# Convolution layer: the 31 taps shared out differently among TensorE, VectorE, ScalarE and GpSimd

## The chip, the core and the metric

The kernel runs on one core of a Trainium2 chip. The metric is the device time of one launch in microseconds; the median of the timed runs counts. Engines are named as in the profile: PE (TensorE, with PEld for its weight loads), DVE (VectorE), ACT (ScalarE), POOL (GpSimd) and SP (which issues the weight DMAs).

## The reference, cut to what matters

The model is six layers over 512 tokens of width 1024: attention, convolution, latent attention, attention, a three-branch mixer and a feed-forward layer. The change lies in the convolution layer alone:

```python
def _conformer_conv(h, w_in, b_in, conv_w, conv_b, ln_g, ln_b, w_out):
    proj = h @ w_in + b_in
    a, b, gate = jnp.split(proj, 3, axis=-1)
    u = a * jax.nn.sigmoid(b)
    u = lax.conv_general_dilated(          # B_CONV = 31 taps, causal, one filter per channel
        u, conv_w[:, None, :].astype(u.dtype), window_strides=(1,),
        padding=[(B_CONV - 1, 0)], dimension_numbers=('NWC', 'WIO', 'NWC'),
        feature_group_count=B_WIDTH) + conv_b
    u = jax.nn.silu(_layer_norm(u, ln_g, ln_b))
    return (u * jax.nn.silu(gate)) @ w_out
```

Each of the 1024 channels is convolved with its own 31 weights, then a layer norm runs over all channels of a token. So nothing of the norm can start before every channel's convolution is done.

## The kernel before

**Arithmetic.** Every large matmul is done in three passes on pairs of rounded halves (`mm3`, high*high, high*low, low*high), all recorded at L195. A weight unit comes by DMA as `wr`; ACT rounds it to `wh` (L53) and, in this layer, POOL subtracts to get the low half `wl` (L60, because `k.share(B_SPLIT)` is 1.0 from the second pair of channels on).

**The convolution layer.** Channels lie on partitions in eight chunks of 128, tokens along the free dimension. `pair(p)` makes `u` for chunks 2p and 2p+1: first the `b` half (sigmoid, L1088), then the `a` half times it (L1093).

- Seven chunks (all but 3) are convolved by `conv(c)`. DVE multiplies and adds tap by tap into a PSUM bank (`tp`, two banks): one L1034 and then n-1 times L1036. The remaining taps are made by ACT as scaled copies (`tmp`, and the first one directly in `acc`, L1040) and added up by POOL (L1042). At the end DVE adds both sums into `y[:, c]` (L1043). n is `B_VECTOR` = 23 for chunks 0 to 6 and `B_LAST` = 20 for chunk 7. The pool has three `acc` and five `tmp` buffers.
- Chunk 3 goes through PE. ACT makes two 128x128 diagonal matrices for each tap (`dh`, `dl`, L1057 and L1058), and PE accumulates 31 taps x 3 matmuls in one bank (`conv_on_tensor`), which ACT copies to `y` with the bias (L1079).

**What sets the order.** A scheduler orders the instructions of each engine ahead of time with a simulated clock: of those ready, the one with the smallest priority number goes first, and each engine then runs its list in that order. Numbers grow along the program. `k.low()` adds a million to them, and `conv(c)` is issued inside it, so a weight split of POOL goes ahead of a tap of the seven chunks. `conv_on_tensor` and the weight stream are outside it.

**After the convolution.** The gate projection (`gates`, 192 matmuls) fills PE while the norm's chain runs. Its order on PE is written out (`manual_schedule`): the channel mean of chunks 0 to 5 (`mean(0, 6)`) comes 22 us of matmul time into the gates, that of chunks 6 and 7 (`mean(6, 8)`) 10 us later, with 24 gate matmuls between the two. After it come `centre` (ACT copies the mean, L1132; DVE and POOL subtract it, L1138 and L1136; ACT squares, L1141; DVE and POOL add, L1150 and L1145), `square` (L1159) and `scale`, each at its place among the gate matmuls.

```python
        flow.later(B_CONV - 10.0, lambda: mean(0, 6))
        flow.later(B_CONV, lambda: mean(6, 8))
        with tc.manual_schedule(engines={mybir.EngineType.PE}):
            for p in range(4):
                k.lin_fm(gates(p))
            flow.need(lambda: "pr" in st)
```

Of the kernel before, what the change touches and what calls it, by code (L numbers as in the profile page):

```python
# [12 lines left out]
AF = mybir.ActivationFunctionType  # L13
ALU = mybir.AluOpType
# [956 lines left out]


B_TAPS = 31
B_VECTOR = 23
B_LAST = 20
B_TENSOR = (3,)
B_CONV = 32.0
B_SQUARE = 7.0
B_POOL = (2, 5)
# [16 lines left out]

def layer_b(k, j, gnext, out=None, on_vector=B_VECTOR, on_tensor=B_TENSOR):
    nc, tc, ins, flow = k.nc, k.tc, k.ins, k.flow
    with ExitStack() as ctx:
# [4 lines left out]
        def wt(n, bufs, nmn, dt=F32):  # L1004
            return work.tile([P, n], dt, tag=nmn, name=k.nm(nmn), bufs=bufs)

        cols, turn1 = k.columns(one, work, [(ins["b_b_in"][j], 24), (ins["b_conv_b"][j], 8), (ins["b_ln_g"][j], 8), (ins["b_ln_b"][j], 8)])
        taps, turn2 = k.tap_columns(one, work, ins["b_conv_w"][j], B_TAPS)
        cb, lg, lb = cols[:, 24:32], cols[:, 32:40], cols[:, 40:48]
# [9 lines left out]
        PAD = 32  # L1019
        u = one.tile([P, 8, PAD + S], F32, tag="u", name=k.nm("u"))  # L1020
        y = one.tile([P, 8, S], F32, tag="y", name=k.nm("y"))
# [5 lines left out]
        tap = lambda a, i: a[:, PAD - B_TAPS + 1 + i : PAD - B_TAPS + 1 + i + S]  # L1027

        def conv(c):

            n = on_vector if c < 7 else B_LAST
            wc = lambda i: taps[:, c, i : i + 1]
            ps = k.bank("tp")
            nc.vector.tensor_scalar(out=ps, in0=tap(u[:, c], 0), scalar1=wc(0), scalar2=cb[:, c : c + 1], op0=ALU.mult, op1=ALU.add)  # L1034
            for i in range(1, n):
                nc.vector.scalar_tensor_tensor(out=ps, in0=tap(u[:, c], i), scalar=wc(i), in1=ps, op0=ALU.mult, op1=ALU.add)  # L1036
            acc = wt(512, 3, "acc")
            for i in range(n, B_TAPS):
                tmp = acc if i == n else wt(512, 5, "tmp")
                nc.scalar.activation(out=tmp, in_=tap(u[:, c], i), func=AF.Copy, scale=wc(i))  # L1040
                if i > n:
                    nc.gpsimd.tensor_tensor(out=acc, in0=acc, in1=tmp, op=ALU.add)  # L1042
            nc.vector.tensor_tensor(out=y[:, c], in0=ps, in1=acc, op=ALU.add)  # L1043

        diag, halves = {}, {}

        def diagonal(c, i):

            if "w" not in halves:
                w = halves["w"] = wt(2 * B_TAPS, 1, "wc").rearrange("p (i n) -> p i n", i=2)  # L1050
                wr = wt(B_TAPS, 1, "wr", F32R)
                nc.scalar.activation(out=wr, in_=taps[:, c], func=AF.Copy)
                nc.vector.tensor_scalar(out=w[:, 0], in0=wr.bitcast(F32), scalar1=1.0, scalar2=None, op0=ALU.mult)
                nc.vector.tensor_tensor(out=w[:, 1], in0=taps[:, c], in1=w[:, 0], op=ALU.subtract)
            w = halves["w"]
            dh, dl = diag[i] = wt(P, 8, "dh", F32R), wt(P, 8, "dl", F32R)
            nc.scalar.activation(out=dh, in_=k.ident, func=AF.Copy, scale=w[:, 0, i : i + 1])  # L1057
            nc.scalar.activation(out=dl, in_=k.ident, func=AF.Copy, scale=w[:, 1, i : i + 1])  # L1058

        def begin_on_tensor(c, ps):  # L1060

            halves["u"] = uh, ul = wt(PAD + S, 1, "uh", F32R), wt(PAD + S, 1, "ul", F32R)
            for a in (uh, ul):
                nc.scalar.activation(out=a[:, 0:PAD], in_=u[:, c, 0:PAD], func=AF.Copy)
            k.split(ps, uh[:, PAD:], ul[:, PAD:])
            with k.low():
                for i in range(8):
                    diagonal(c, i)

        def conv_on_tensor(c):  # L1070

            uh, ul = halves["u"]
            ps = k.bank("lin")
            for i in range(B_TAPS):
                if i not in diag:
                    diagonal(c, i)
                k.mm3(ps, *diag[i], tap(uh, i), tap(ul, i), i == 0, i == B_TAPS - 1)
                flow.pump()
            nc.scalar.activation(out=y[:, c], in_=ps, func=AF.Identity, bias=cb[:, c : c + 1])  # L1079

        def pair(p):
            sig = {}

            def on_b(c, ps):
                flow.need(lambda: ready)
                sig[c] = wt(512, 3, "sig")
                i = 8 + 2 * p + c
                k.table("sig", nc.scalar.activation(out=sig[c], in_=ps, func=AF.Sigmoid, bias=cols[:, i : i + 1]))  # L1088

            def on_a(c, ps):  # L1090
                i = 2 * p + c
                dst = ps if i in on_tensor else u[:, i, PAD:]
                nc.vector.scalar_tensor_tensor(out=dst, in0=ps, scalar=cols[:, i : i + 1], in1=sig[c], op0=ALU.add, op1=ALU.mult)  # L1093
                if i in on_tensor:
                    begin_on_tensor(i, ps)
                else:
                    with k.low():
                        conv(i)

            return [(k.h_opnd, 8, on_b), (k.h_opnd, 8, on_a)]  # L1100
# [15 lines left out]
        for c in on_tensor:  # L1116
            conv_on_tensor(c)
# [4 lines left out]
        def mean(a, b):  # L1122
            if a == 0:
                st["pm"] = k.bank("sc")
            for c in range(a, b):
                k.mm(st["pm"], ones, y[:, c], c == 0, c == 7)
            if b == 8:
                centre()
# [38 lines left out]
# [4 lines that stand above are left out]
# [514 lines left out]
```

## Time and profile before

| | us |
|---|---|
| median of 3 runs | 2039.26 (2038.92 to 2047.69) |
| the profiled execution: its time | 2043.2 |
| its span, first to last instruction | 2041.4 |
| the convolution's taps in it, first to last POOL add | 345.3 to 459.8 |
| layer norm and the rest of the gates | up to about 492 |

The profile is of one execution, so its stretches are compared with its own span. Times in the rows are us from the start of the span, and ns where a mean is given. A busy PE is not a PE at its peak, since matmuls overlap: what counts is how far apart they start.

### The profile page before, as it was taken

Reading aid. Unit: us, or ns where it says so; the run is one execution under the profiler, and the core shown is the slowest. Engines: PE = TensorE matmul, PEld = TensorE weight load, DVE = VectorE, ACT = ScalarE, POOL = GpSimd, SP = SyncE. Lnnn points to the kernel's source line nnn. Section 1 sums busy time; section 2 is a strip of 40 time slices with the busy share of each in tenths; the row PEclk is TensorE's granted clock in tenths of the full one; section 3 lists DMA queues with packets and bytes.
Section 4 is the critical chain, followed back from the end, with each engine's and each line's share of the span. In section 5 each row is a group of like instructions: output and inputs, shape, how many; then the busy total and the mean of one; then the engine's idle time right before and its main releaser. Section 6 shows DMA issues by size and latency. Waiting matters only on the chain.

```text
span 2041.4 us, 27224 instructions
## 1 busy us (share of the span) xinstructions
PE 1988.7 (97%) x9875; PEld 1663.7 (81%) x9875; DVE 1172.4 (57%) x2185; ACT 996.7 (49%) x2107; POOL 915.0 (45%) x812
## 2 busy tenths in 40 slices
PE   8999999999999999999999999999999999999999
PEld 6787888887898887877778888888888888888887
DVE  6677766995456656786665678747624433221321
ACT  5555646574465645555554776546423333222220
POOL 6666624993455417775535444102511223333331
PEclk9899999999999999999999999999999999999999
DMA  6122142323331323221423122322334244333331
GB/s 199 45 83 83 42 145 89 122 62 116 106 100 43 104 74 107 65 83 42 140 88 100 59 82 73 93 83 69 118 102 136 93 125 144 93 100 97 100 96 52
DMA packets 161095, 191.54 MB, mean 94 GB/s; under 512 B 15917, under 2 KB 131997, under 8 KB 160960
## 3 DMA queue, kind: packets, MB, share of 16 engines
q1 hardware_dynamic: 160960, 189.80, 29.6%
q8 instruction: 78, 1.28, 0.3%
q14 instruction: 57, 0.47, 0.1%
HBM read 177.18 MB, written 12.58 MB: 93 GB/s over the span
## 4 chain that ended last, share of the span: by engine, by line
PE 81%; DVE 6%; POOL 5%; ACT 3%; issue 2%; DMA 2%; SPq 0%; DVEq 0%; ACTq 0%; POOLq 0%
PE lin L195 71%; PE sc L195 4%; PE tp L195 3%; PE tp L303 2%; DVE wl L60 1%; POOL st L217 1%; PE lin L303 1%; POOL wl L60 1%; DMA wr<-in_a_w_in_dram 1%; POOL m L461 1%; ACT wh L53 1%; POOL m L460 1%; DVE m L580 1%; DVE st L644 0%; ACT w L638 0%
## 5 line engine op out<-in xcount | busy, mean ns | idle before, releaser
L60 POOL TENSOR_TENSOR wl<-wr,wh 128x1024 fp32r<-128x1024 f32 (+2 forms) x151 | 364.8, 2420 | 506.4 <-ACT wh L53 490.9
L53 ACT ACTIVATE wh<-wr 128x1024 fp32r<-128x1024 f32 (+2 forms) x306 | 318.6, 1044 | 376.1 <-PE lin L195 230.7
L195 PE MATMUL lin<-hh,wh 128*128 128x512 f32 (+1 forms) x928 | 350.1, 379 | 3.3 <-ACT hh L353 3.3
L195 PE MATMUL lin<-hl,wh 128*128 128x512 f32 (+1 forms) x928 | 350.1, 378 | 0.0
L195 PE MATMUL lin<-hh,wl 128*128 128x512 f32 (+1 forms) x928 | 349.2, 377 | 0.0
L195 PE MATMUL lin<-wh,hh 128*128 128x512 f32 (+2 forms) x864 | 332.9, 387 | 1.9 <-DVE sg L602 0.7
L195 PE MATMUL lin<-wl,hh 128*128 128x512 f32 (+2 forms) x864 | 329.2, 382 | 1.1 <-DVE wl L60 1.1
L195 PE MATMUL lin<-wh,hl 128*128 128x512 f32 (+2 forms) x864 | 330.1, 382 | 0.1
L60 DVE TENSOR_TENSOR wl<-wr,wh 128x1024 fp32r<-128x1024 f32 (+3 forms) x155 | 211.4, 1367 | 188.9 <-ACT wh L53 188.1
L195 PEld LDWEIGHTS lin<-hh,wh 128*128 128x128 f32 x928 | 175.7, 190 | 35.3 <-ACT hh L353 3.6
L195 PEld LDWEIGHTS lin<-hl,wh 128*128 128x128 f32 x928 | 175.9, 190 | 31.6 <-issue 0.5
L195 PEld LDWEIGHTS lin<-hh,wl 128*128 128x128 f32 x928 | 175.9, 190 | 31.2
L195 PEld LDWEIGHTS lin<-wh,hh 128*128 128x128 f32 x864 | 165.0, 191 | 29.0 <-PE tp L303 0.9
L195 PEld LDWEIGHTS lin<-wl,hh 128*128 128x128 f32 x864 | 165.2, 191 | 27.8 <-DVE wl L60 2.2
L195 PEld LDWEIGHTS lin<-wh,hl 128*128 128x128 f32 x864 | 164.8, 191 | 27.2 <-DVE hl L354 0.4
L195 PE MATMUL lin<-wh,ot 128*128 128x512 f32 x384 | 129.9, 404 | 1.2 <-ACT ot L680 1.0
L217 POOL TENSOR_TENSOR st<-st,minus_half 128x8 f32<-128x8 f32 (+4 forms) x109 | 115.5, 1061 | 7.6 <-DVE st L1159 2.3
L468 DVE TENSOR_TENSOR x<-lin,x 128x512 f32<-128x512 f32 x80 | 54.3, 687 | 102.3 <-PE lin L195 101.9
L1036 DVE SCALAR_TENSOR_TENSOR tp<-u,taps,tp 128x512 f32<-128x512 f32 x151 | 104.0, 754 | 1.1
L638 ACT ACTIVATE w<-sc,st 128x128 f32<-128x128 f32 (+3 forms) x128 | 67.0, 524 | 71.8 <-DVE st L637 71.0
L195 PEld LDWEIGHTS lin<-wh,ot 128*128 128x128 f32 x384 | 71.3, 188 | 16.1 <-ACT ot L680 2.1
L1042 POOL TENSOR_TENSOR acc<-acc,tmp 128x512 f32<-128x512 f32 x52 | 66.7, 1301 | 22.4 <-ACT tmp L1040 21.4
(321 smaller groups left out, 3814.8 us busy)
## 6 DMA issues: line engine op xcount, KB each, us to landing
wr<-in_a_w_in_dram SPq DMA_DIRECT2D x128, 256.0 KB
wr<-in_w_in_dram SPq DMA_DIRECT2D x48, 512.0 KB
wr<-in_b_w_in_dram SPq DMA_DIRECT2D x24, 512.0 KB
wr<-in_w_branch_dram SPq DMA_DIRECT2D x24, 512.0 KB
wr<-in_w_ffn_gate_dram SPq DMA_DIRECT2D x22, 512.0 KB
wr<-in_w_ffn_up_dram SPq DMA_DIRECT2D x22, 512.0 KB
wr<-in_w_ffn_down_dram SPq DMA_DIRECT2D x22, 512.0 KB
xs<-x SPq DMA_DIRECT2D x40, 256.0 KB
```

What stands on the lines that cost most here:

```text
L53: nc.scalar.activation(out=hi, in_=raw, func=AF.Copy)
L60: eng.tensor_tensor(out=lo, in0=raw, in1=hi.bitcast(F32), op=ALU.subtract)
L195: self.nc.tensor.matmul(out=out, lhsT=lhsT, rhs=rhs, start=start, stop=stop)
L217: self.nc.gpsimd.tensor_tensor(out=y, in0=ms, in1=self.minus_half.to_broadcast(list(ms.shape)), op=ALU.pow)
L303: self.nc.tensor.transpose(tp[:, c], a, self.ident)
L460: nc.gpsimd.tensor_tensor(out=mv, in0=rv, in1=bc(cs), op=ALU.mult)
L461: nc.gpsimd.tensor_tensor(out=m, in0=m, in1=tmp, op=ALU.add)
L468: self.nc.vector.tensor_tensor(out=xs, in0=ps, in1=xs, op=ALU.add)
L580: nc.vector.tensor_tensor(out=mv, in0=mv, in1=r.unsqueeze(2).to_broadcast([P, 8, 64]), op=ALU.mult)
L638: nc.scalar.activation(out=e[:, m, :n], in_=sc[:, :n], func=AF.Exp, bias=mx[:, m : m + 1], accum_out=sums[:, 2 * m + h : 2 * m + h + 1],)
L1036: nc.vector.scalar_tensor_tensor(out=ps, in0=tap(u[:, c], i), scalar=wc(i), in1=ps, op0=ALU.mult, op1=ALU.add)
L1042: nc.gpsimd.tensor_tensor(out=acc, in0=acc, in1=tmp, op=ALU.add)
```

## The change

TensorE's chunk gets 24 taps as diagonals instead of 31. The other seven are made as for the other chunks, by ACT and POOL: `rest(c, n)` is the old ACT and POOL loop of `conv` as a function, called for chunk 3 outside `k.low()`. For that the chunk's `u` is needed in SBUF too, so ACT copies it from the bank. The last step of chunk 3 is now one DVE instruction that adds bank, bias and `acc`. The seven other chunks lose a tap on DVE each (23 to 22, and 20 to 19 for chunk 7), which goes to ACT and POOL.

```diff
-B_VECTOR = 23
-B_LAST = 20
+B_VECTOR = 22
+B_LAST = 19
 B_TENSOR = (3,)
+B_DIAGONAL = 24
...
             for i in range(1, n):
                 nc.vector.scalar_tensor_tensor(out=ps, in0=tap(u[:, c], i), scalar=wc(i), in1=ps, op0=ALU.mult, op1=ALU.add)
+            nc.vector.tensor_tensor(out=y[:, c], in0=ps, in1=rest(c, n), op=ALU.add)
+
+        def rest(c, n):
+
             acc = wt(512, 3, "acc")
             for i in range(n, B_TAPS):
                 tmp = acc if i == n else wt(512, 5, "tmp")
-                nc.scalar.activation(out=tmp, in_=tap(u[:, c], i), func=AF.Copy, scale=wc(i))
+                nc.scalar.activation(out=tmp, in_=tap(u[:, c], i), func=AF.Copy, scale=taps[:, c, i : i + 1])
                 if i > n:
                     nc.gpsimd.tensor_tensor(out=acc, in0=acc, in1=tmp, op=ALU.add)
-            nc.vector.tensor_tensor(out=y[:, c], in0=ps, in1=acc, op=ALU.add)
+            return acc
...
             k.split(ps, uh[:, PAD:], ul[:, PAD:])
+            nc.scalar.activation(out=u[:, c, PAD:], in_=ps, func=AF.Copy)
...
-            for i in range(B_TAPS):
+            acc = rest(c, B_DIAGONAL)
+            for i in range(B_DIAGONAL):
                 if i not in diag:
                     diagonal(c, i)
-                k.mm3(ps, *diag[i], tap(uh, i), tap(ul, i), i == 0, i == B_TAPS - 1)
+                k.mm3(ps, *diag[i], tap(uh, i), tap(ul, i), i == 0, i == B_DIAGONAL - 1)
                 flow.pump()
-            nc.scalar.activation(out=y[:, c], in_=ps, func=AF.Identity, bias=cb[:, c : c + 1])
+            nc.vector.scalar_tensor_tensor(out=y[:, c], in0=ps, scalar=cb[:, c : c + 1], in1=acc, op0=ALU.add, op1=ALU.add)
```

## Rows read from the trace of the kernel before

**Rows 1.** The page's busy times by engine: us, share of the span, instructions.

```profile
PE 1988.7 (97%) x9875; PEld 1663.7 (81%) x9875; DVE 1172.4 (57%) x2185; ACT 996.7 (49%) x2107; POOL 915.0 (45%) x812
```

**Rows 2.** Chain that ended last, convolution to norm: start, length, what.

```profile
459.93 5.15 PE sc L195 x12
465.07 5.50 PE lin L195 x24
470.57 1.72 PE sc L195 x4
...
479.43 1.24 POOL acc L1145
```

**Rows 3.** Windows over the taps: length, busy time of each engine, clock.

```profile
345.33:459.78 114.45, 114.45 (x518) 94.83 (x517) 110.95 (x165) 79.50 (x137) 110.73 (x72) 1.00 0.28 88
```

**Rows 4.** Groups on POOL, DVE and ACT in that stretch: count, busy, mean.

```profile
L1042 POOL TENSOR_TENSOR acc<-acc,tmp 128x512 f32<-128x512 f32 x52 | 66.7, 1301 | 22.4 <-ACT tmp L1040 21.4
L60 POOL TENSOR_TENSOR wl<-wr,wh 128x1024 fp32r<-128x1024 f32 x20 | 48.2, 2415 | 1.6 <-ACT wh L53 1.6
L1043 DVE TENSOR_TENSOR y<-tp,acc 128x512 f32<-128x512 f32 x7 | 4.8, 687 | 0.1
L1040 ACT ACTIVATE tmp<-u,taps 128x512 f32<-128x512 f32 x52 | 35.7, 713 | 4.5 <-POOL acc L1042 4.3
```

**Rows 5.** Timeline of PE: first taps of chunk 3, the two means, the square.

```profile
414.16 0.39 PE L195 MATMUL lin<-uh,dh 128*128 128x512 f32 x1
414.39 0.39 PE L195 MATMUL lin<-ul,dh 128*128 128x512 f32 x1
...
480.71 1.95 PE L195 MATMUL sc<-ones,acc 128*128 128x1 f32 x16 [0.90 <-POOL acc L1145]
```

**Rows 6.** Timeline of POOL: one double split, then the end of the taps.

```profile
352.95 4.79 POOL L60 TENSOR_TENSOR wl<-wr,wh 128x1024 fp32r<-128x1024 f32 x2
...
425.97 14.47 POOL L1042 TENSOR_TENSOR acc<-acc,tmp 128x512 f32<-128x512 f32 x11 [1.13 <-ACT tmp L1040]
...
455.75 4.03 POOL L1042 TENSOR_TENSOR acc<-acc,tmp 128x512 f32<-128x512 f32 x3
459.73 2.37 POOL L60 TENSOR_TENSOR wl<-wr,wh 128x1024 fp32r<-128x1024 f32 x1
469.47 2.37 POOL L60 TENSOR_TENSOR wl<-wr,wh 128x1024 fp32r<-128x1024 f32 x1 [7.37 <-ACT wh L53]
```

**Rows 7.** Timeline of DVE: a run of taps, and the last two sums.

```profile
352.25 15.24 DVE L1036 SCALAR_TENSOR_TENSOR tp<-u,taps,tp 128x512 f32<-128x512 f32 x23
...
455.24 0.69 DVE L1043 TENSOR_TENSOR y<-tp,acc 128x512 f32<-128x512 f32 x1
...
464.62 0.69 DVE L1043 TENSOR_TENSOR y<-tp,acc 128x512 f32<-128x512 f32 x1
```

**Rows 8.** Timeline of ACT: two diagonals, chunk 3's `y`, a weight.

```profile
415.08 0.39 ACT L1057 ACTIVATE dh<-ident,wc 128x128 fp32r<-128x128 f32 x1
415.38 0.39 ACT L1058 ACTIVATE dl<-ident,wc 128x128 fp32r<-128x128 f32 x1
...
444.05 0.69 ACT L1079 ACTIVATE y<-lin,cols 128x512 f32<-128x512 f32 x1 [2.16 <-PE lin L195]
...
468.33 1.06 ACT L53 ACTIVATE wh<-wr 128x1024 fp32r<-128x1024 f32 x1 [9.01 <-PE lin L195]
```

**Rows 9.** Timeline of PE after an idle stretch at the layer's start, 256 columns.

```profile
320.07 1.22 PE L195 MATMUL lin<-hh,wh 128*128 128x256 f32 x4 [3.35 <-ACT hh L353]
...
325.51 0.29 PE L195 MATMUL lin<-hh,wh 128*128 128x256 f32 x1
325.64 0.28 PE L195 MATMUL lin<-hl,wh 128*128 128x256 f32 x1
```

**Rows 10.** Windows around that stretch and the square; the clock stands third from the end.

```profile
322.00:324.00 2.00, 2.00 (x11) 2.00 (x10) 0.91 (x2) 1.05 (x2) 1.08 (x3) 0.50 0.85 252
484.00:486.00 2.00, 2.00 (x6) 1.60 (x5) 0.23 (x1) 0.96 (x1) 0.00 (x0) 0.51 0.18 43
```

## The prediction

> **What bounds the kernel now.** I read the busy times first: PE is busy for 97% of the span, so time is won only where PE has less to do or waits less [rows 1]. Then the chain that ended last. Through the convolution layer it runs on PE alone, over the first mean, 24 gate matmuls and the second mean, and leaves PE only behind that, in the norm, where POOL's last sum of squares holds up the square for 0.90 us [rows 2, 5]. So in this layer PE sets the time up to the second mean.
>
> Then the windows: between POOL's first and last tap lie 114.45 us, of which POOL works 110.73 and DVE 110.95; ACT has 35 us free, POOL 3.7 [rows 3]. This is the view that matters: two engines beside PE are as good as full. The groups say with what: POOL makes 52 tap sums and splits 19 weights (the 20th starts 0.05 us before the stretch ends) [rows 4, 6]. Last the ends: POOL's last tap ends at 459.78, DVE's last sum at 465.31 [rows 6, 7], while PE reads chunk 7 only with the second half of the second mean. That mean takes 1.72 us from 470.57, two chunks of 0.86, so chunk 7 is wanted at 471.43 [rows 2]. The reader is to see that the convolution has 6.1 us to spare there today, and that no wait appears because of it.
>
> **PE.** 7 taps x 3 = 21 matmuls go. In the tap stretch they start 0.23 us apart [rows 5], so 21 x 0.23 = 4.8 us, and all of it lies on the chain: PE comes to the second mean 4.8 us earlier and wants chunk 7 at 471.43 - 4.8 = 466.6. If everything else is in time, this is the whole change: -4.8 us.
>
> **DVE.** Seven taps go. 23 in a row take 15.24 us with the last one's full length in it, so one costs 0.66 us and seven 4.6 [rows 7]. The new last step of chunk 3 adds one instruction; the nearest row is the last sum of a chunk, one bank and one SBUF operand, 0.69 us [rows 4]. DVE gains 3.9 us: its own share would be ready when PE comes.
>
> **ACT.** 14 diagonals go at 0.30 us apart (4.2 us) and chunk 3's 0.69 us copy to `y` [rows 8]. To be added: the copy of `u`, about 0.69 by the same row, and 14 scaled copies of at most 0.71, together 10.6 [rows 4]. Net 5.7 us more, against 35 us free: hidden, as long as ACT doesn't stand in its own queue behind a copy that waits for a `tmp` buffer. Before that cost ACT 4.3 us in all [rows 4].
>
> **POOL.** Here I see the price. Sums before: 6 chunks x 7 + 10 = 52, as the row counts. After: 6 chunks of 9 ACT taps give 48, chunk 7 with 12 gives 11, chunk 3 with 7 gives 6: 65, so 13 more. Two splits in a row take 4.79, one alone 2.42 or less, so one slot is 2.37 us [rows 6]; 19 of them are 45.0 of POOL's 110.73, and the other 65.7 over 52 sums make 1.263 each [rows 3, 4]. 13 x 1.263 = 16.4 us.
>
> The GPSIMD Engine Reference of the Trainium skill (section 4.1, Engine selection) speaks against this move: it gives two-input arithmetic to VectorE and calls GpSimd about twice as slow. Here the rows show 1301 ns on POOL against 687 ns on DVE for a sum of the same size, a ratio of 1.9 [rows 4]. With the page's measured ratio of 1.96 (section 3.1) on the 687 ns, 13 sums would be estimated at 17.5 us instead of 16.4, and the forecast would come out 1.1 us later.
>
> Where do these 16.4 us go? POOL has 3.7 us of gaps in the stretch. Weight splits have the smaller priority number and go ahead of the seven chunks' sums. As POOL's end moves back, two more splits fall in front of it: the one at 459.73, and the one at 469.47, which hangs on a weight rounding of ACT at 468.33, and that on PE's progress [rows 6, 8]; it comes 4.8 us earlier with PE. The one after that needs PE to pass the second mean, so it can't come in between. POOL's last tap then ends at 459.78 + 16.4 + 2 x 2.37 - 3.7 = 477.2 if it fills every gap, and chunk 7 is there after DVE's sum, 0.69 + 0.1 later: 478.0. PE wants it at 466.6, so it stands for 11.4 us; against before chunk 7's mean starts 478.0 - 471.4 = 6.6 us later.
>
> Bounds: if the second split does not get in front, POOL ends at 474.8 (+4.2 instead of +6.6); if the same 3.7 us of gaps remain, at 480.9 (+10.3). I take the middle since POOL has sums waiting at every moment. Where the scheduler puts chunk 3's six sums (early, I expect, as they aren't low and its `u` is made with the second pair) doesn't matter for the end: the work is the same.
>
> **The clock after the stall.** The trace has no idle of PE as long as this. The nearest row is 3.35 us at the start of the layer. From 320.07 matmuls of 256 columns started at half the pace until 325.5, with a granted clock of 0.50, 1.2 GHz, in the window; from then on 0.13 apart [rows 9, 10]. So about 5.4 us at half pace after the stall. Chunk 7's part of the mean takes 1.7 instead of 0.86: +0.9. In the 3.7 us that are left about 8.6 gate matmuls start 0.43 instead of 0.23 apart: +1.7, of which 0.9 goes into the wait that PE has before the square anyway [rows 5]: +0.8. Bounds: zero if the clock stays up. And the square of before was itself followed by matmuls at 0.51 [rows 10], six in 2 us where at full pace nine would start; if the clock is higher there, up to 1.6 us come back.
>
> **Sum.** 6.6 + 0.9 + 0.8 = +8.3 us; the norm behind the mean is unchanged and moves as a whole. On the profiled span, 2041.4 + 8.3 = 2049.7, and 2051.5 with the 1.8 us around it. That execution took 2043.2, 3.9 more than the median of the runs, so on the median it is 2039.26 + 8.3 = 2047.6. From the bounds (+4.2 without the clock and 1.6 back: +2.6; +10.3, the clock and some 2 us of reordering in later layers, estimated from the size of the gaps here: +14) the case reaches from 2041.9 to 2053.3.
>
> **Rivals.**
>
> 1. *It pays (faster).* The place is POOL's queue between 345 and 466. For it: POOL is often ahead of DVE; the eleven sums in a row that end at 440.44 are the last 2 of chunk 5, 7 of chunk 6 and 2 of chunk 7, and DVE closes chunk 6 only at 455.24 and chunk 7 at 464.62 [rows 6, 7]. If POOL's last tap ended by 465.8, PE would not wait and the 4.8 us stood: 2034.4. It decides where POOL needs 11.4 us less than I count: two thirds of the added sums would have to cost nothing. Against it: the gaps are 3.7 us, and being ahead of DVE is no spare time in an engine that is never idle. Chance 0.12.
>
> 2. *Buffers and queues make it worse.* Chunk 3's `acc` is one of three and is held from its first copy until PE's last diagonal, near 444 - 4.8. The seven chunks would then have two, and ACT, which runs its list in order, would stand more often behind a copy without a buffer. At each of the later four chunks POOL would wait for ACT's first two copies, at most 2 x 0.71 = 1.4 us, so 5.7 us; POOL's end 482.9, and the time 2047.6 + 5.7 = 2053.3. Against it: with POOL late, DVE is no longer what frees an `acc` last, so the next chunk's copies are made while POOL still sums the one before. It decides if POOL shows more than some 4 us of gaps in the stretch. Chance 0.18.
>
> 3. *TensorE's chunk is not what ends late.* Should chunk 3's seven taps be put behind those of the other chunks, the first mean waits for them, 4.8 us before the second. PE would stall in two places, but the end of POOL's work is the same, so the time is that of the forecast; it is in its chance.
>
> **How the numbers follow.** Forecast (POOL's end holds up the second mean) 0.65, first rival 0.12, second 0.18, other 0.05 (a reordering of later layers, either way). 0.5% is 10.2 us, about what a measurement of this kernel can tell from no change: 2029.1 to 2049.5. The first rival lies within it. Of the forecast about a fifth lies above (0.13), of the second rival nearly all (0.16): slower 0.29. Faster needs more than the whole 4.8 us: 0.02. Same 0.69. The range 2034 to 2054 holds the first rival, the forecast and over half of the second.
>
> **What would show it.** In the profile after: 72 diagonal matmuls on PE in place of 93; 65 sums at L1042 and its like, of 1.3 us each; POOL busy without a gap from 345 to about 477; DVE's last sum of chunk 7 at about 478 instead of 465.3, directly behind POOL; a PE wait of about 11 us in front of the second mean where there was none, and a clock of 0.5 after it. The prediction is wrong if PE shows no wait at the mean (then the time is about 2034), if the splits are put behind the sums and PE waits for weights instead, or if POOL's end is right and the stall is made up later.

## The result, and the profile after

The kernel became slower: 2063.43 us (median of 6 runs, 2062.44 to 2064.88) against 2040.8 for the kernel before on the same chips (6 runs, 2038.92 to 2047.69), a ratio of 1.0105 [1.0091, 1.012]. That is outside the predicted range. The profiled execution took 2063.18 us with a span of 2061.4, 20.0 more than before.

The page's busy times of the kernel after, as [rows 1]:

```profile
PE 1987.3 (96%) x9854; PEld 1659.9 (81%) x9854; DVE 1172.4 (57%) x2179; ACT 1002.4 (49%) x2107; POOL 932.9 (45%) x825
```

PE has its 21 matmuls less, POOL 13 instructions and 17.9 us more; the work is what the prediction counted. So the 20 us are time in which PE stands. PE's timeline at the first mean:

```profile
454.86 2.74 PE L195 MATMUL sc<-y,ones 128*128 128x512 f32 x6
477.55 5.36 PE L195 MATMUL sc<-y,ones 128*128 128x512 f32 x6 [19.96 <-DVE y L1086]
```

This is the first mean, not the second: PE does its part for chunks 0 to 2 at 454.86, then stands for chunk 3, whose last step is now L1086 on DVE. The chain that ended last, as [rows 2], starts from that step:

```profile
476.75 0.76 DVE y L1086
477.51 0.04 issue
477.55 5.36 PE sc L195 x6
482.92 5.49 PE lin L195 x24
488.41 1.72 PE sc L195 x4
...
498.55 2.54 PE sc L195 x16
501.09 5.33 PE lin L195 x12
506.42 1.02 PE sc L195 x8
```

The 24 gate matmuls started at 465.07 before and start at 482.92 now, 17.85 us later; the second mean and the square are late by the same 17.84. The rest of the first mean took 5.36 us instead of half of 5.15. The windows show why, and also where another 1.5 us go behind the square (clock third from the end):

```profile
478.00:484.00 6.00, 6.00 (x12) 2.77 (x12) 0.00 (x0) 0.00 (x0) 0.00 (x0) 0.61 0.00 0
500.00:506.00 6.00, 6.00 (x18) 4.94 (x18) 0.39 (x2) 1.06 (x1) 2.42 (x2) 0.50 0.33 71
```

Why is chunk 3 so late? POOL's timeline at the end of the taps, as [rows 6], and DVE's two last sums, as [rows 7]:

```profile
454.06 2.37 POOL L60 TENSOR_TENSOR wl<-wr,wh 128x1024 fp32r<-128x1024 f32 x1
456.40 20.31 POOL L1047 TENSOR_TENSOR acc<-acc,tmp 128x512 f32<-128x512 f32 x16
487.31 2.37 POOL L60 TENSOR_TENSOR wl<-wr,wh 128x1024 fp32r<-128x1024 f32 x1 [10.60 <-ACT wh L53]
```

```profile
472.85 0.69 DVE L1038 TENSOR_TENSOR y<-tp,acc 128x512 f32<-128x512 f32 x1 [6.88 <-POOL acc L1047]
...
476.75 0.75 DVE L1086 SCALAR_TENSOR_TENSOR y<-lin,cols,acc 128x512 f32<-128x512 f32 x1 [3.21 <-POOL acc L1047]
```

POOL's last 16 sums, up to 476.71, are by their count those of chunks 7 and 3 (the other six chunks have 48 of the 65, and 49 come before); DVE closes chunk 7 at 472.85 and chunk 3 at 476.75, behind it. The amount is as counted (groups and window of the tap stretch, as [rows 4] and [rows 3]): 65 sums, and gaps of 131.38 - 128.91 = 2.5 us.

```profile
L1047 POOL TENSOR_TENSOR acc<-acc,tmp 128x512 f32<-128x512 f32 x65 | 82.5, 1287 | 23.2 <-ACT tmp L1045 22.3
```

```profile
345.33:476.71 131.38, 112.27 (x502) 91.84 (x501) 114.27 (x165) 85.46 (x137) 128.91 (x85) 0.94 0.26 81
```

Not for want of data: ACT's timeline shows chunk 3's copy of `u` (L1071) at 373.55, but the first copy into its `acc` at 444.67, behind those of chunk 6 (419.89) and chunk 7 (431.25). DVE's closing sum of chunk 5, which frees an `acc`, ends at 443.93 + 0.69 = 444.62.

```profile
373.55 0.60 ACT L1071 ACTIVATE u<-lin 128x512 f32<-128x512 f32 x1 [0.76 <-DVE ul L354]
...
419.89 0.71 ACT L1045 ACTIVATE acc<-u,taps 128x512 f32<-128x512 f32 x1
...
431.25 0.71 ACT L1045 ACTIVATE acc<-u,taps 128x512 f32<-128x512 f32 x1
...
444.67 0.71 ACT L1045 ACTIVATE acc<-u,taps 128x512 f32<-128x512 f32 x1
```

```profile
443.93 0.69 DVE L1038 TENSOR_TENSOR y<-tp,acc 128x512 f32<-128x512 f32 x1
```

In the program, `rest` for chunk 3 comes after `conv` of the last pair. The theory from here on: the three `acc` and five `tmp` buffers are handed out in program order, so that chunk 3, though its priority number is the smaller, gets an `acc` only after chunk 7 has one. The rival: chunk 3's place costs nothing in itself, as the prediction has it, and the added sums of POOL cost about this much wherever they stand.

### The profile page after: what moved, and what is told of

It is laid out like the page before. It is cut to its first block, busy times and chain, and to the rows that moved or that the text cites. A ratio compares the mean times of both kernels' runs of the same rounds, so it can differ in the third digit from the quotient of the medians.

```text
span 2061.4 us, 27191 instructions
## 1 busy us (share of the span) xinstructions
PE 1987.3 (96%) x9854; PEld 1659.9 (81%) x9854; DVE 1172.4 (57%) x2179; ACT 1002.4 (49%) x2107; POOL 932.9 (45%) x825
## 4 chain that ended last, share of the span: by engine, by line
PE 65%; DVE 4%; POOL 4%; issue 2%; ACT 2%; DMA 0%; SPq 0%; POOLq 0%; DVEq 0%; ACTq 0%
PE lin L195 57%; PE sc L195 3%; PE tp L195 2%; PE tp L303 2%; POOL wl L60 1%; PE lin L303 1%; POOL st L217 1%; DVE wl L60 1%; POOL m L461 1%; DVE m L580 0%; POOL m L460 0%; DVE rl L1389 0%; DMA wr<-in_a_w_in_dram 0%; ACT w L638 0%; DVE st L637 0%
## 5 line engine op out<-in xcount | busy, mean ns | idle before, releaser
L1047 POOL TENSOR_TENSOR acc<-acc,tmp 128x512 f32<-128x512 f32 x65 | 82.5, 1287 | 23.2 <-ACT tmp L1045 22.3
```

## The experiments

Ratios are against the kernel before, run on the same chip; its medians were 2043.16, 2044.47 and 2044.0 in the three groups of runs (up to 1.3 us apart, and 2040.8 beside the result above, so ratios are compared). "Layer's end" is DVE's first addition to `x` behind the gates: 514.2 us before and 533.7 after.

**Chunk 3 in buffers of its own.** Its sum goes straight into `y[:, 3]`, its scaled copies into two halves of another tile. Nothing else is changed; the calls and priorities are those of the kernel after.

```diff
-        def rest(c, n):
+        def rest(c, n, own=False):
-            acc = wt(512, 3, "acc")
+            acc = y[:, c] if own else wt(512, 3, "acc")
+            two = work.tile([P, 2, 512], F32, tag="w4", name=k.nm("two"), bufs=1) if own else None
-                tmp = acc if i == n else wt(512, 5, "tmp")
+                tmp = acc if i == n else two[:, i % 2] if own else wt(512, 5, "tmp")
-            acc = rest(c, B_DIAGONAL)
+            acc = rest(c, B_DIAGONAL, True)
```

> The change whole, but chunk 3's seven taps get buffers of their own: they are added up in the chunk's own y, and the scaled copies go through the two halves of a tile that is free by then. Theory A (acc and tmp buffers are handed out in the order of the program, so that chunk 3, called after all pairs, gets its first one only when chunk 7 has its own, and the first mean waits for POOL's last sum): POOL now makes chunk 3's sums between 375 and 425, the first mean does not wait, the second waits about 11 us for chunk 7, and the time is that of my prediction, 6 to 10 us above the kernel before: 2047 to 2051. Rival B (the scheduler puts chunk 3 last whatever its buffers): nothing moves, about 2063. Rival C (the amount of POOL's work alone sets the end, whichever mean waits): about 2063 too, although chunk 3 is early.

Measured: 2052.76 us, ratio 1.004 [1.0028, 1.0052], layer's end 524.2. POOL's timeline, chunk 3's first and last sum and the end:

```profile
380.10 1.29 POOL L1048 TENSOR_TENSOR y<-y,two 128x512 f32<-128x512 f32 x1
...
413.01 1.31 POOL L1048 TENSOR_TENSOR y<-y,two 128x512 f32<-128x512 f32 x1
...
465.56 2.36 POOL L60 TENSOR_TENSOR wl<-wr,wh 128x1024 fp32r<-128x1024 f32 x1
467.88 11.88 POOL L1048 TENSOR_TENSOR acc<-acc,tmp 128x512 f32<-128x512 f32 x9
```

And PE's two means:

```profile
455.32 5.31 PE L195 MATMUL sc<-y,ones 128*128 128x512 f32 x12
...
469.92 2.08 PE L195 MATMUL sc<-y,ones 128*128 128x512 f32 x2 [3.79 <-DVE y L1038]
480.54 2.07 PE L195 MATMUL sc<-y,ones 128*128 128x512 f32 x2 [8.55 <-DVE y L1038]
```

Buffers alone move chunk 3's sums from the end of POOL's work to its middle. The first mean goes through in one piece, and PE waits at the second: 3.79 us for chunk 6 and 8.55 for chunk 7. This is the predicted kernel: two splits in front, POOL's end at 479.8 (477.2 forecast), 12.3 us of waits (11.4 forecast), +0.40%, which by this ratio is 8.2 us (8.3 forecast). That the last two agree so well is partly luck: at the layer's end this kernel is 10.0 us late, and the layers behind it give some of that back.

**Another order of the mean.** The kernel after, with chunk 3 moved to the second mean; POOL's work stays as it is.

```diff
-            for c in range(a, b):
-                k.mm(st["pm"], ones, y[:, c], c == 0, c == 7)
+            for c in ((0, 1, 2, 4, 5) if a == 0 else (6, 7, 3)):
+                k.mm(st["pm"], ones, y[:, c], c == 0, c == 3)
```

> The change whole, chunk 3 still last on POOL, but the first mean takes chunks 0, 1, 2, 4, 5 and the second 6, 7 and 3. Theory A: nothing but the last third of the second mean waits for chunk 3, the gate matmuls and the mean parts that stood behind the wait go ahead of it, and the time falls by some 13 us from 2063 to 2048 to 2052. Rival C: the wait only changes its place, 2063.

Measured: 2051.46 us, ratio 1.0038 [1.0025, 1.0051], layer's end 524.1. PE's timeline:

```profile
455.90 4.45 PE L195 MATMUL sc<-y,ones 128*128 128x512 f32 x10
...
466.37 1.02 PE L195 MATMUL sc<-y,ones 128*128 128x512 f32 x2
477.81 2.07 PE L195 MATMUL sc<-y,ones 128*128 128x512 f32 x2 [10.42 <-DVE y L1038]
481.78 2.08 PE L195 MATMUL sc<-y,ones 128*128 128x512 f32 x2 [1.89 <-DVE y L1086]
```

And POOL's end:

```profile
467.10 13.83 POOL L1047 TENSOR_TENSOR acc<-acc,tmp 128x512 f32<-128x512 f32 x11
```

POOL even ends 4.2 us later than in the kernel after (467.10 + 13.83 = 480.93), since one more split, at 464.75, comes in front of its last sums; what PE does before it stands has changed. With the mean of five chunks, the 24 gate matmuls and chunk 6's mean ahead of the wait, it is 12.3 us instead of 20.0 (10.42 of it for chunk 7, only 1.89 for chunk 3), and the kernel is about 0.67% (1.0105 against 1.0038) faster. The rival, that chunk 3's place costs nothing, falls by both runs. Two different cures bring the same.

**Each half of the change alone.** First: 24 diagonals, with the other chunks' taps as before (`B_VECTOR = 23`, `B_LAST = 20`). Then: 31 diagonals, with a tap less on DVE in each chunk (the kernel before with 22 and 19).

> Half of the change: 24 diagonals and chunk 3's other seven taps by ACT and POOL (6 more sums, 7.6 us), but the seven chunks keep 23 and 20 taps on DVE. Theory A: POOL ends at 466 to 468.5, chunk 3 is again its last and is there at about 468; the first mean wants it at 457.7 and waits about 10 us, and the clock falls behind the wait: 9 to 11 us above the kernel before, 2050 to 2052. Had only POOL's amount against the second mean counted, it would be about even with the kernel before, 2039 to 2043.

> The other half: all 31 taps of chunk 3 as diagonals, one tap less on DVE for each of the seven chunks (7 more sums on POOL, 8.8 us). POOL ends at 467 to 470, the second mean wants chunk 7 at 471.4, so no wait and the time of the kernel before, within 3 us: 2038 to 2044. If POOL's end alone decided, it would be later by up to the 8.8 us: 2049.

Diagonals alone: 2051.72 us, ratio 1.0038 [1.0025, 1.0051]. PE's timeline:

```profile
453.36 2.74 PE L195 MATMUL sc<-y,ones 128*128 128x512 f32 x6
467.93 4.33 PE L195 MATMUL sc<-y,ones 128*128 128x512 f32 x6 [11.83 <-DVE y L1086]
```

Six sums more are enough for a wait of 11.83 us, since chunk 3 is again POOL's last and the first mean wants it. The time is 7.8 us up by the ratio, less than the 9 to 11 forecast; the layer's end is 5.7 us late. Taps alone: 2047.3 us, 1.0017 [1.0007, 1.0026], that is 3.5 us by the ratio, where no wait and at most 3 us were forecast. PE waits 2.40 us at the second mean:

```profile
474.09 1.12 PE L195 MATMUL sc<-y,ones 128*128 128x512 f32 x2 [2.40 <-DVE y L1043]
```

The forecast of POOL's end for that run (467 to 470) was early: it was 473.3, with splits at 459.1 and 469.7 in front of the last sum.

**Diagonals alone, chunk 3 in its own buffers.** 24 diagonals, 23 and 20 taps on DVE, and the first experiment's edit.

> 24 diagonals, chunk 3's seven taps in buffers of their own, the seven chunks at 23 and 20 taps on DVE as before, all splits on POOL. Against the run with the same work and shared buffers (7.8 us above the kernel before) only the place of chunk 3 in the order differs. If the order is what cost there: POOL ends near 469 (467.1, and the second split comes in front), chunk 7 is there at 470, PE wants it at 466.6 and waits some 3.5 us at the second mean only; 2 us below to 3 us above the kernel before. If the sums' amount cost it, the time stays 8 us above.

Measured: 2042.42 us, ratio 0.9995 [0.9986, 1.0004]; layer's end 515.6 against 519.9 with the shared buffers. The first mean has no wait, the second one of 5.50 us:

```profile
455.72 5.31 PE L195 MATMUL sc<-y,ones 128*128 128x512 f32 x12
...
472.89 2.08 PE L195 MATMUL sc<-y,ones 128*128 128x512 f32 x2 [5.50 <-DVE y L1038]
```

The same work in the same number of instructions, 0.43% apart. Of the 9.6 us between the two spans, 4.3 arise in this layer; the others come up in the layers behind it, and I did not follow them. The wait that is left is not POOL's alone: POOL's last sum ends at 471.71 and DVE's last tap at 472.04, both later than the 469 forecast for POOL.

**Splits taken from POOL.** If POOL's amount is what is left to pay, a quarter or 15% of its splits on DVE should help: `B_SPLIT = 0.75` with the own buffers, then 0.85, then 0.85 in the kernel just shown (23 and 20 taps), and 0.75 in the kernel before.

```diff
-B_SPLIT = 1.0
+B_SPLIT = 0.75
```

> The change whole with chunk 3's taps in buffers of their own (as in the run before it), and one weight split in four given to DVE (B_SPLIT 0.75). If POOL's amount of work is what is left of the loss: five splits less make POOL end near 468 instead of 479.8, DVE with five more of 1.2 us ends near 467.4, PE wants chunk 7 at 466.7, so its wait falls from 12.3 us to 1 to 3 and the 4.8 us of fewer matmuls begin to show: 1 to 4 us below the kernel before. If something else held PE (the order, the queue of ACT), the time stays near that run's, 8 us above.

> The same with B_SPLIT 0.85, three splits on DVE. POOL ends near 472.7, PE waits about 6 us, between the two: 1 to 4 us above the kernel before. A step of the wait in proportion to the splits moved says that POOL's queue sets it.

> 24 diagonals with buffers of their own for chunk 3, the seven chunks at 23 and 20 taps on DVE as before, B_SPLIT 0.85. POOL ends near 462, DVE, which keeps its taps and gets three splits and chunk 3's last sum, near 469.5: now DVE is late, PE waits about 3 us, 1 to 3 us below the kernel before.

> The kernel before with B_SPLIT 0.75 alone. There POOL holds up nothing in front of the means, so freeing it gives nothing; DVE gets 6 us and ends near 471.3, just when PE wants chunk 7: within 2 us of the kernel before. If it is faster by more than 3 us, a gain of the run with 0.75 would not be the change's.

All four missed and were slower: 2057.24 us (1.0059 [1.0042, 1.0076]), 2060.51 (1.0072 [1.0057, 1.0087]), 2054.76 (1.0044 [1.0029, 1.0059]) and 2051.66 (1.0028 [1.0013, 1.0042]). In the first three, one split on DVE took 14 to 18 us. With 0.75 and own buffers, DVE's, POOL's and ACT's timelines:

```profile
401.21 17.59 DVE L60 TENSOR_TENSOR wl<-wr,wh 128x1024 fp32r<-128x1024 f32 x1
```

```profile
416.43 1.29 POOL L1048 TENSOR_TENSOR acc<-acc,tmp 128x512 f32<-128x512 f32 x1
...
432.78 2.37 POOL L60 TENSOR_TENSOR wl<-wr,wh 128x1024 fp32r<-128x1024 f32 x1 [15.05 <-ACT wh L53]
```

```profile
431.03 0.72 ACT L1046 ACTIVATE acc<-u,taps 128x512 f32<-128x512 f32 x1 [16.16 <-DVE y L1038]
```

DVE's taps stand behind the split, so the chunk's sum comes late, and with it the release of an `acc`; ACT, which runs its list in order, stands 16.16 us behind a copy that has none, and the diagonals behind that copy come late too. PE's waits show both:

```profile
PE lin L195 <- ACT dh L1063: 11.9, 1, 11.9
...
PE sc L195 <- DVE y L1038: 4.5, 1, 4.5
```

Work taken from the full engine was put on one that couldn't do it beside that engine. In the kernel before, with 0.75, no split on DVE took more than 2.37 us, and PE waits 2.3 us at the mean. Its ten runs spread from 2045.32 to 2057.44, and the profile is of one of the quick ones (2047.48), so it does not show what made the median 0.28% longer.

**Where the balance lies.** Own buffers, 23 and 20 taps on DVE, splits on POOL, `B_DIAGONAL` 27 and 28.

> The same with 27 diagonals: four taps of chunk 3 leave PE (12 matmuls, 2.8 us) and give POOL three sums (3.8 us). PE wants chunk 7 at 468.6; POOL ends near 465 and DVE's last sum at 466.1, so nothing waits and PE's 2.8 us are won: 1 to 3.5 us below the kernel before. If it is not faster, what PE saves is lost behind the means.

> 28 diagonals: three taps, 9 matmuls (2.1 us) less, two sums more on POOL. No wait in front of either mean, 1 to 3 us below the kernel before.

Measured: 2039.57 us, ratio 0.9975 [0.9965, 0.9985], and 2041.86, 0.9986 [0.9977, 0.9995]. Both ratios lie clear of 1; the first is the fastest kernel of all. Its means on PE:

```profile
457.90 5.31 PE L195 MATMUL sc<-y,ones 128*128 128x512 f32 x12
468.55 1.02 PE L195 MATMUL sc<-y,ones 128*128 128x512 f32 x2
471.71 1.12 PE L195 MATMUL sc<-y,ones 128*128 128x512 f32 x2 [2.14 <-DVE y L1038]
```

A wait of 2.14 us was left where I had expected none, since DVE closed chunk 7 at 470.96, later than I had worked out, 5.0 us after POOL's last sum (459.30 + 6.69 = 465.99):

```profile
459.30 6.69 POOL L1048 TENSOR_TENSOR acc<-acc,tmp 128x512 f32<-128x512 f32 x5
```

```profile
470.96 0.69 DVE L1038 TENSOR_TENSOR y<-tp,acc 128x512 f32<-128x512 f32 x1
```

By the ratio the gain is 5.1 us, more than the 1 to 3.5 forecast. The layer's end is 513.1, 1.0 us earlier than before; the span is 5.9 shorter. So most of that gain arises behind this layer, by a cause I have not found; the gain as a whole is measured, its place is not. The kernel with 28 diagonals says the same from the other side: 2.9 us by the ratio, as forecast, with a wait of 0.44 us and a layer's end of 512.3, earlier than with 27. A few us of the whole time can't be put down to this layer.

## Why the prediction was wrong

**What failed.** In the part on POOL: "Where the scheduler puts chunk 3's six sums [...] doesn't matter for the end: the work is the same." And with it the third rival, which named the case that came ("should chunk 3's seven taps be put behind those of the other chunks, the first mean waits") but gave it the forecast's time. POOL's end is indeed the same, but what counts is what PE has left to do when it stands. At the second mean, a wait to 478.0 would have left one chunk's mean behind it. At the first mean, the wait to 477.55 leaves three chunks' mean, the 24 gate matmuls and the second mean behind it. The working lacked a term: three chunks' mean (2.6 us), 24 gates (5.5) and chunk 6's mean (0.9), 9.0 together, lie ahead of the wait in the forecast and behind it here; the wait is 20.0 instead of 11.4, 8.6 more. The forecast has the layer +8.3 us late and it is +19.5: 8.4 of these 11.2 us are the place of the wait (+15.0 instead of +6.6) and 2.6 the price of the clock (+4.3 instead of +1.7), both as below.

From the rows, before to after: chunk 3's part of the first mean starts at 477.55 instead of 459.93 + 2.57 = 462.5, so +15.0; the rest of that mean takes 5.36 instead of 2.57, +2.8; this makes the 17.8 that the gates, the second mean and the square show. The scale starts 7.87 us behind the square (506.42 - 498.55), where it was 6.40 before (487.11 - 480.71, the square's start in [rows 5]): 1.5 more, and the layer's end is at +19.5.

**Why chunk 3 was last.** I expected its sums early because of their priority number. The number orders what is ready, and a copy with no `acc` isn't. Own buffers, with calls and numbers unchanged, moved the sums from 456 to 477 up to 380 to 414; so the shared buffers were the cause. Whether the three `acc` or the five `tmp` did it was not taken apart. That the buffers go round in the order of the calls fits the order of the first copies (chunks 6, 7, 3), and chunk 3's starts right after chunk 5 has freed its `acc`; ACT was busy up to it, so no row shows the wait itself, and a call of `rest` for chunk 3 ahead of the other chunks was not tried.

**What was right.** *PE:* 72 diagonal matmuls, and PE comes to the first mean at 454.86 instead of 459.76, 4.9 us earlier (4.8 forecast). *POOL:* its last sum ends at 476.71 (477.2 forecast), though by another sum: 2.5 us of gaps, 1287 ns a sum, and one split in front instead of two, because the second hangs on PE beyond the first mean, where PE now stood; with the order of the first experiment it came in front, at 465.56. That the end came so close is luck: the split that is missing takes 2.4 us off, and the 2.5 us of gaps, where none were forecast, put as much on. In the first experiment, with both splits, 3.1 us of gaps were left and the end was 2.6 us late, so "if it fills every gap" was too hopeful. *ACT:* its extra work is hidden; the second rival's gaps on POOL aren't there. *The mechanism and its size:* POOL is the full engine, its end is later than PE wants, and PE waits: in the two runs of the whole change where PE waits at the second mean alone (own buffers, other order of the mean), 12.3 us of waits, layer's end +10.0 and +9.9, time +0.40% and +0.38%, against +8.3 us forecast.

**The clock.** The kind was right, the size was that of the wrong place. After 19.96 us of standing PE was granted 0.61 over the 6 us from 478 (0.50, that is 1.2 GHz, up to 482, and 1.00, 2.4 GHz, from 484), and three chunks' mean paid for it, +2.8, instead of one chunk's mean and some gates, +0.9 and +0.8. The 1.6 us that might come back behind the square didn't: there the clock was 0.50 from 500 to 506, against 0.72 from 482 to 488 before, and 1.5 more were lost. Why it stayed low for longer there is open.

## What to carry to other kernels

Taking work from the bound engine pays only as long as the engine that gets it has time before its result is wanted; read that as a slack in us (6.1 here) and charge the whole moved work to it (16.4 here). Ask not only when the last of a queue ends but which result is last, and who wants that one first: the same POOL work, with another chunk last or another order of the reader, was worth 0.65 to 0.67%. And a part whose result is wanted early should not take its buffers from a pool shared with parts that are called before it and wanted later.

## What the runs showed of the hardware that I had not expected

A weight split on DVE, two operands in SBUF, takes 1.21 us when POOL isn't at work (the kernel before, first row below). Beside a POOL that works without gaps it took 17.59, 16.78 and 14.03 us in three runs. Each time it ended 1.08 or 1.09 us after POOL's first gap began: in the first 418.80 against 416.43 + 1.29 = 417.72, in the second 424.93 against 423.84, in the third 421.44 against 420.35. Here are the second's rows of DVE and POOL, behind that of the kernel before:

```profile
499.45 1.21 DVE L60 TENSOR_TENSOR wl<-wr,wh 128x1024 fp32r<-128x1024 f32 x1
```

```profile
408.15 16.78 DVE L60 TENSOR_TENSOR wl<-wr,wh 128x1024 fp32r<-128x1024 f32 x1
```

```profile
422.56 1.28 POOL L1048 TENSOR_TENSOR acc<-acc,tmp 128x512 f32<-128x512 f32 x1
...
437.69 2.53 POOL L1048 TENSOR_TENSOR acc<-acc,tmp 128x512 f32<-128x512 f32 x2 [13.84 <-ACT tmp L1046]
```

A pause of POOL isn't always needed. Of the splits on DVE beside POOL's taps in these three runs, nine more took 1.30 to 2.37 us and one 5.86. They, too, ended 1.08 or 1.09 us after the end of a POOL instruction, but POOL's next one followed at once or 0.08 us later, and was itself 0.8 to 1.0 us longer than usual. In the first run a split ends at 382.21, 1.08 us after a sum of POOL ends at 381.13, and the next sum takes 2.27 us instead of 1.29:

```profile
380.70 1.51 DVE L60 TENSOR_TENSOR wl<-wr,wh 128x1024 fp32r<-128x1024 f32 x1
```

```profile
379.84 1.29 POOL L1048 TENSOR_TENSOR y<-y,two 128x512 f32<-128x512 f32 x1
381.10 3.53 POOL L1048 TENSOR_TENSOR acc<-acc,tmp 128x512 f32<-128x512 f32 x2
```

So the two don't do this work at the same time: between two instructions of POOL either the split goes first and POOL's next one stands, or POOL goes on and the split stands. The three long ones were passed over until POOL ran out of work; it did so because ACT, which feeds it, stood 16.16, 15.08 and 11.74 us for a result of DVE from behind the split. Which of the two goes first between two instructions, the runs show no rule for.

DVE's taps, whose second operand is a bank, go on beside a busy POOL at 0.66 us each [rows 7]. The Trainium skill (SBUF — State Buffer, section SBUF: two separate sides) says that GpSimd and a DVE operation with two SBUF inputs share a port pair as "an exclusive lock, not a bandwidth split", held for one whole instruction by whichever starts first. The runs agree that one blocks the other, both ways; but in the first long case the block lasted while POOL began and ended ten instructions more, not one. That the lock is the cause was not isolated: a split on DVE without a second SBUF operand was not tried. In the kernel before with splits on DVE, where POOL worked 106.44 of 129.67 us, the longest was 2.37 us.
